# When SyncE asks for V tiles, U tiles and gates in the last stage of a decoder block's expert layer

## The chip, the cores and the metric

The kernel runs on one core of a Trainium2 chip, as one launch. The metric is the device time of that launch in microseconds (us), the median of three runs. Engines are named as the profile does: PE is TensorE, DVE VectorE, ACT ScalarE, POOL GpSimd, SP SyncE. Here SP does nothing but issue transfers, in the order of its program: an issue that waits for a buffer holds all that stand behind it. POOL gathers rows from DRAM (indirect DMAs, on a queue of its own). All transfers share 16 DMA engines.

## The reference

One block of a hybrid decoder on 512 tokens of width 1024: three token mixers side by side (an attention with forget gates, a sliding-window attention and a memory attention), merged by gates and projected, and then a layer of 128 x 128 = 16384 single-neuron experts, of which each token uses 16 for each of 8 heads. The last part is what matters here:

```python
x = x + merged @ w_out[l]
x = x + peer_ffn(rmsnorm(x, norm2_g[l]), ...)
# in peer_ffn, for each token c and its 128 chosen experts e_c, with gates g_c:
a = jnp.einsum('cd,ced->ce', h_c, u[e_c])
act = jax.nn.gelu(a, approximate=False) * g_c
return jnp.einsum('ce,ced->cd', act, v[e_c])
```

## The kernel before

The 512 tokens are four blocks of 128. Blocks 0 and 1 do the experts by rows: POOL fetches the rows of u, and later of v, that each token chose (L833, one row of 4 KB a token, 128 tokens at a time), and DVE multiplies them with the token (L843, tile `scr`) or adds them up weighted (L852, tile `mg`). Blocks 2 and 3 (256 tokens) do the experts densely, over all 16384, in 128 tiles of 128 experts each:

- a U tile (`dense_u`, 512 KB of uT): PE multiplies it with the tokens and ACT takes the gelu into `ga`, the activations of that tile. Two of three U tiles go to PE as plain fp32 (L968). The third is "split": ACT casts it to fp32r (`uhi`, L955), DVE takes the rest (`ulo`, L957), and PE does three cheaper passes.
- the gates of a tile: DVE multiplies `ga` by them (L1079). Those of tiles 0 to 31 stay in SBUF and are multiplied in as they arise; those of the other tiles are written to DRAM (`gd`) and read back four tiles at a time into `gq` (L1061), of which there are two buffers.
- a V tile (`dense_v`, 512 KB of peer_v, into `raw` or, for every fourth, `last`): ACT casts it (`whi`, L1084) and the activations (`ah`, L1082), DVE takes the rests (`wlo`, L128, and `al`, L1087), and PE adds 12 matmuls of 512 columns to four accumulators (tiles `sc` and `tp`, L142 to L144).

The last stage, "beside V", is the loop over k = 0 to 127 in which V tile k is multiplied. Before it 57 or 58 of the U tiles are done; the others are spread over the loop, and so are the remaining row steps of blocks 0 and 1 (`step()`). An iteration runs the first half of `operands(k + 1)` (loads, gates, casts), begins a U tile where one is due, does row steps, takes `ulo` of a split U tile, runs the second half of `operands` (`wlo`, `al`), multiplies the U tile begun one iteration earlier and asks for the U tile three ahead, and multiplies V tile k. There are four buffers for V loads: tile k + 4 takes that of tile k, which is free once `wlo` of tile k has been computed. U tiles have three buffers, all in the tile `hhi` in this stage. The order on POOL, DVE and PE is that of the program from the dense part on (`manual_schedule`, L996 in the kernel before); that on ACT, and before the change that on SP, is chosen by the scheduler of the tile framework.

Of the kernel before, what the change touches and what calls it, by code (L numbers as in the profile page):

```python
# [36 lines left out]
U_SPLIT = 3  # L37
VFAR = 3
PLAIN_ROWS, V_EARLY = 12, 5
GQ_AT, GQ_PARTS = 0, 4  # L40
RAW_MORE = 5
STEPS_U = 4
SPARE, STEPS_N = 4, 0.8
# [4 lines left out]
GK = 4  # L48
# [8 lines left out]
def tile_block(ctx: ExitStack, tc: tile.TileContext, t: dict, out: bass.AP):  # L57
# [61 lines left out]
    def rest(loaded, pool):  # L119
        raw, hi, n, c = loaded  # L120
        w = raw.shape[1]
        lo = wp.tile([128, WSLOT], F32R, tag="wlo", name="wlo")[:, :w]
        due[0] += pool
        if due[0] >= 1.0:
            due[0] -= 1.0
            G.tensor_tensor(lo, raw, hi.bitcast(F32), op=OP.subtract)
        else:
            V.tensor_sub(lo, raw, hi.bitcast(F32))  # L128
        if c > 1:
            return [x.rearrange("p (c n w) -> p n c w", c=c, n=n) for x in (hi, lo)]  # L130
        return [x.rearrange("p (n w) -> p n w", n=n) for x in (hi, lo)]
# [790 lines left out]
    def ga(k):  # L922
        s = k % (LAG + 1)
        return soon[:, s] if s <= LAG - GA_LATE else late[0][:, s - (LAG + 1 - GA_LATE)]
# [21 lines left out]
    def dense_u(k):  # L946

        if k < FIRST_U:
            w = load_raw(t["uT"][k], D)[:, :D]
        else:  # L950
            fetch_u_to(min(k + URING - 1, LAG + 1) if k < LAG else k)
            w = u_raw.pop(k)
        if split_u(k):
            hi, lo = (gp[0].tile([128, D], F32R, tag=tag, name=tag, bufs=1) for tag in ("uhi", "ulo"))
            A.copy(hi, w)  # L955
            yield
            V.tensor_sub(lo, w, hi.bitcast(F32))  # L957
            yield
            ps, hi, lo = bank("mm"), *(x.rearrange("p (n w) -> p n w", n=KC) for x in (hi, lo))
            for dc in range(KC):  # L960
                mm3(ps[:, :TD], (hi[:, dc], lo[:, dc]), [x[dc] for x in h2s], dc == 0, dc == KC - 1)
            A.activation(ga(k), ps[:, :TD], AF.Gelu)
            return
        w = w.rearrange("p (n w) -> p n w", n=KC)
        yield
        ps = bank("mm")
        for dc in range(KC):
            PE.matmul(ps[:, :TD], w[:, dc], h2f[dc], start=dc == 0, stop=dc == KC - 1)  # L968
            yield
        A.activation(ga(k), ps[:, :TD], AF.Gelu)  # L970
# [80 lines left out]
    def get_gates(k, part):  # L1051

        k -= k % GK
        if not KEPT <= k < NK or not 0 <= part < GQ_PARTS:
            return
        if part == 0:
            gq["raw"] = gp[0].tile([128, ND, 128 // TG, GK * TG], F32, tag="gq", name="gq")
            gq[k] = gq["raw"].rearrange("p i g (k t) -> p (i g) k t", k=GK)
        n = ND * (128 // TG) // GQ_PARTS
        i, g = divmod(part * n, 128 // TG)  # L1060
        nc.sync.dma_start(gq["raw"][:, i, g:g + n], gd[i][:, g:g + n, k * TG:(k + GK) * TG])  # L1061

    def fetch_v(k):
        if k < NK:
            pool, n = (gp[0], 1) if k % SPARE == SPARE - 1 else (wp, None)
            tag = "last" if n else "raw"
            raw = pool.tile([128, D if n else WSLOT], F32, tag=tag, name=tag, **({"bufs": n} if n else {}))
            v_raw[k] = raw[:, :D]
            nc.sync.dma_start(v_raw[k], t["peer_v"][k * NK:(k + 1) * NK])

    def operands(k):

        fetch_v(k + VFAR)
        get_gates(k + GK, k % GK - GQ_AT)
        raw, a = v_raw.pop(k), ga(k)
        if k >= KEPT:
            m = gq[k - k % GK][:, :, k % GK]
            g = a.rearrange("p (g t) -> p g t", t=TG)
            V.tensor_mul(g, m, g)  # L1079
        ah = gp[0].tile([128, TD], F32R, tag="ah", name="ah")  # L1080
        al = gp[0].tile([128, TD], F32R, tag="al", name="al")
        A.copy(ah, a)  # L1082
        hi = wp.tile([128, WSLOT], F32R, tag="whi", name="whi")[:, :D]
        A.copy(hi, raw)  # L1084
        yield
        w = [x[:, 0] for x in rest((raw, hi, 1, 1), 0.0)]
        V.tensor_sub(al, a, ah.bitcast(F32))  # L1087
        yield w, ah, al

# [65 lines left out]
    while k_u < LAG:  # L1155
        list(dense_u(k_u))
        k_u += 1
    start, ready = done[0], list(operands(0))[1]
    assert start >= 2 * NJ
    nc.sync.dma_start(out[0:128], x1[0])  # L1160
# [5 lines left out]
    for k in range(NK):  # L1166
        now, coming, us = ready, operands(k + 1) if k + 1 < NK else None, begun
        if coming:
            next(coming)
        begun = []  # L1170
        while k_u < min(NK, LAG + (NK - LAG) * (k + 1) // (NK - 5)):
            begun.append((dense_u(k_u), k_u))
            next(begun[-1][0])
            k_u += 1
        while done[0] < min(len(JOBS), start + (len(JOBS) - start) * (k + 1) // (NK - 4)):
            step()
        for u, n in begun:
            if split_u(n):
                next(u)
        ready = next(coming) if coming else None  # L1180
        for u, n in us:
            list(u)
            fetch_u_to(n + URING_V)
        dense_v(k, *now)
# [96 lines left out]
```

## Time and profile before

| what | us |
|---|---|
| median of three runs | 1624.09 (1624.01 to 1626.73) |
| the profiled execution, its own time | 1624.32 |
| its span on the chip | 1622.5 |
| PE busy | 1545.8 (95%) |
| DVE busy | 1394.1 (86%) |
| ACT busy | 769.1 (47%) |
| POOL busy | 790.5 (49%) |

The mean granted clock of PE was 0.981. The transfers moved 531.83 MB at a mean of 328 GB/s; SP's queue and POOL's moved nearly all of it, 249.12 and 268.47 MB. Busy shares are means over stages with different limits, so they are read by stage; the last stage runs from about 1005 us to the end. A row of the timeline gives the start, the duration, the engine, the line and the operation, and in brackets how long the engine had been idle before it and what released it. "SPq" rows are issues of transfers: the duration is that of the issue, not of the transfer.

### The profile page before, as it was taken

To read this page: it belongs to the slowest core of one execution; us is meant where nothing else is said; L and a number is where in the kernel's file an instruction comes from. 1 tells how busy PE (TensorE), PEld (TensorE's weight loads), DVE (VectorE), ACT (ScalarE), POOL (GpSimd) and SP (SyncE) were. 2 spreads that over 40 slices of the span, in tenths; PEclk is the share of its full clock that TensorE was granted. 3 is DMA by queue.
4 is the path that set the end of the run, shared out by engine and by line. 5 is a ranking of instruction groups with operands and counts; after the bars stand their busy time and mean duration, and the time that the engine had idled before them with its cause. 6 is when DMAs were issued, how large, how long until landed. Compare 5 with 4: busy or idle time off the path is not lost.

```text
span 1622.5 us, 26255 instructions
## 1 busy us (share of the span) xinstructions
PE 1545.8 (95%) x8934; PEld 1382.1 (85%) x8934; DVE 1394.1 (86%) x2709; ACT 769.1 (47%) x1770; POOL 790.5 (49%) x625
## 2 busy tenths in 40 slices
PE   6999999999998989987999999899999999998998
PEld 5999899998887988987888998688888888887887
DVE  5677358899988999999998999788899888897987
ACT  7787337645445434543117878333333333333332
POOL 1100012767556555678553332566555555555652
PEclk9999999999998999999999999999999999999999
DMA  7586743899998899867997999999999999999995
GB/s 298 197 276 219 252 162 131 319 356 319 339 317 296 294 345 347 291 212 258 348 393 286 362 386 335 402 399 379 390 397 402 397 400 402 401 401 401 383 400 220
DMA packets 178101, 531.83 MB, mean 328 GB/s; under 512 B 18224, under 2 KB 47152, under 8 KB 177968
## 3 DMA queue, kind: packets, MB, share of 16 engines
q0 software_dynamic: 73728, 268.47, 44.4%
q1 hardware_dynamic: 100784, 249.12, 42.1%
q10 hardware_dynamic: 3456, 12.58, 2.0%
q8 instruction: 70, 1.15, 0.3%
q14 instruction: 63, 0.52, 0.1%
HBM read 515.42 MB, written 14.68 MB: 327 GB/s over the span
## 4 chain that ended last, share of the span: by engine, by line
PE 51%; DMA 17%; issue 14%; POOL 9%; DVE 8%; ACT 2%; SPq 0%; POOLq 0%; DVEq 0%; ACTq 0%
PE mm L968 15%; DMA row<-in_peer_v_dram,eidx 9%; POOL row L833 8%; PE mm L143 5%; PE mm L142 5%; PE mm L144 5%; DMA row<-in_peer_u_dram,eidx 3%; PE mm L295 2%; DVE wlo L128 2%; DVE scr L843 2%; PE sc L1038 2%; PE tp L1038 2%; PE sc L143 1%; PE sc L144 1%; PE tp L144 1%
## 5 line engine op out<-in xcount | busy, mean ns | idle before, releaser
L833 POOL DMA_INDIRECT row<-in_peer_v_dram,eidx x256 | 351.2, 1372 | 280.8 <-DVE mg L852 157.3
L833 POOL DMA_INDIRECT row<-in_peer_u_dram,eidx x256 | 334.9, 1308 | 266.4 <-DVE scr L843 155.0
L128 DVE TENSOR_TENSOR wlo<-raw,whi 128x1024 fp32r<-128x1024 f32 (+1 forms) x243 | 305.7, 1259 | 44.4 <-ACT whi L116 34.9
L843 DVE SCALAR_TENSOR_TENSOR scr<-row,own 128x1024 bf16<-128x1024 f32 x256 | 314.5, 1229 | 23.1 <-DMA row<-in_peer_u_dram,eidx 20.1
L852 DVE SCALAR_TENSOR_TENSOR mg<-row,acts,mg 128x1024 f32<-128x1024 f32 x237 | 304.4, 1284 | 10.7 <-DMA row<-in_peer_v_dram,eidx 6.8
L968 PE MATMUL mm<-h2f,hhi 128*128 128x256 f32 x1168 | 266.3, 379 | 0.0
L968 PEld LDWEIGHTS mm<-h2f,hhi 128*128 128x128 f32 x1168 | 218.9, 190 | 30.0
L116 ACT CAST whi<-raw 128x1024 fp32r<-128x1024 f32 (+1 forms) x148 | 154.8, 1049 | 93.7 <-PE mm L143 38.7
L189 POOL TENSOR_TENSOR rsy<-rsv,mhalf 128x4 f32<-128x4 f32 (+5 forms) x25 | 39.3, 1576 | 218.2 <-DVE rsv L188 126.2
L1084 ACT CAST whi<-raw 128x1024 fp32r<-128x1024 f32 x96 | 100.5, 1047 | 71.5 <-DMA raw<-in_peer_v_dram 50.1
L142 PE MATMUL sc<-whi,ah 128*128 128x512 f32 x256 | 110.7, 433 | 11.3 <-ACT ah L1082 6.7
L142 PE MATMUL mm<-hhi,whi 128*128 128x384 f32 x320 | 111.1, 348 | 8.0 <-ACT ga L970 6.8
L970 ACT ACTIVATE ga<-mm 128x256 f32<-128x256 f32 x95 | 36.4, 383 | 172.0 <-PE mm L968 165.7
L143 PE MATMUL mm<-hlo,whi 128*128 128x384 f32 x320 | 111.5, 348 | 0.0
L144 PE MATMUL mm<-hhi,wlo 128*128 128x384 f32 x320 | 110.6, 346 | 0.0
L142 PE MATMUL mm<-whi,hhi 128*128 128x256 f32 (+1 forms) x360 | 104.6, 292 | 3.0 <-DVE g L572 1.9
L143 PE MATMUL sc<-wlo,ah 128*128 128x512 f32 x256 | 102.2, 399 | 4.6 <-DVE wlo L128 4.6
L143 PE MATMUL mm<-wlo,hhi 128*128 128x256 f32 (+1 forms) x360 | 103.1, 287 | 0.9 <-DVE wlo L128 0.9
L1082 ACT CAST ah<-ga 128x256 fp32r<-128x256 f32 x116 | 46.7, 405 | 118.6 <-PE tp L143 73.8
L144 PE MATMUL sc<-whi,al 128*128 128x512 f32 x256 | 102.3, 399 | 0.0
L144 PE MATMUL mm<-whi,hlo 128*128 128x256 f32 (+1 forms) x360 | 101.8, 285 | 0.0
L142 PE MATMUL tp<-whi,ah 128*128 128x512 f32 x256 | 101.4, 396 | 0.0
(289 smaller groups left out, 3780.7 us busy)
## 6 DMA issues: line engine op xcount, KB each, us to landing
hhi<-in_uT_dram SPq DMA_DIRECT2D x96, 512.0 KB
raw<-in_peer_v_dram SPq DMA_DIRECT2D x96, 512.0 KB
raw<-in_w_tr_dram SPq DMA_DIRECT2D x48, 512.0 KB
raw<-in_w_nat_dram SPq DMA_DIRECT2D x40, 512.0 KB
last<-in_peer_v_dram SPq DMA_DIRECT2D x32, 512.0 KB
raw<-in_w_o_dram SPq DMA_DIRECT2D x24, 512.0 KB
hlo<-in_uT_dram SPq DMA_DIRECT2D x24, 512.0 KB
gd<-st ACTq DMA_DIRECT2D x24, 512.0 KB
```

What stands on the lines that cost most here:

```text
L116: A.copy(hi[:, :n * w], raw[:, :n * w])
L128: V.tensor_sub(lo, raw, hi.bitcast(F32))
L142: PE.matmul(ps, lh, rh, start=first, stop=False)
L143: PE.matmul(ps, lh, rl, start=False, stop=False)
L144: PE.matmul(ps, ll, rh, start=False, stop=last)
L833: G.indirect_dma_start(out=r, out_offset=None, in_=t["peer_" + tab], in_offset=bass.IndirectOffsetOnAxis(ap=eidx[b][:, j:j + 1], axis=0))
L843: V.scalar_tensor_tensor(scr, r, 1.0, h2n[b], op0=OP.mult, op1=OP.mult, accum_out=acts[b][:, c]))
L852: V.scalar_tensor_tensor(x1[b], r, acts[b][:, c], x1[b], op0=OP.mult, op1=OP.add))
L968: PE.matmul(ps[:, :TD], w[:, dc], h2f[dc], start=dc == 0, stop=dc == KC - 1)
L1038: PE.matmul(ps[:, u], o[:, 1, u], o[:, 0, u], start=True, stop=True)
L1082: A.copy(ah, a)
L1084: A.copy(hi, raw)
```

## The change

```diff
-GQ_AT, GQ_PARTS = 0, 4
+GQ_PARTS = 2
...
     def operands(k):
 
-        fetch_v(k + VFAR)
-        get_gates(k + GK, k % GK - GQ_AT)
+        if k % GK == 0:
+            for part in range(GQ_PARTS):
+                get_gates(k + GK, part)
         raw, a = v_raw.pop(k), ga(k)
...
         w = [x[:, 0] for x in rest((raw, hi, 1, 1), 0.0)]
+        fetch_v(k + VFAR + 1)
         V.tensor_sub(al, a, ah.bitcast(F32))
         yield w, ah, al
...
+    ctx.enter_context(tc.manual_schedule(engines={mybir.EngineType.Pool, mybir.EngineType.DVE, mybir.EngineType.PE,
+                                                  mybir.EngineType.SP}))
+    fetch_v(VFAR)
     start, ready = done[0], list(operands(0))[1]
```

`VFAR` is 3 and `GK` is 4. From the start of the last stage SP, too, issues in program order. A V tile's load stands right after the `wlo` (`rest`) that frees its buffer, instead of at the head of `operands` of the tile after. The gates of a group of four tiles are read by two transfers of 256 KB (one for each token block) at the head of the group before, instead of by four of 128 KB, one in each of the four iterations of the program; the bytes and the buffers are the same. PE's, DVE's and POOL's orders are unchanged.

SP's order at the start of the stage, from the load of V tile 2 on. `raw` and `last` are V tiles (2, 3, 4, ...), `hhi` are U tiles, `gq` gates. Before:

```order
L1069 DMA raw_10752<-in_peer_v_dram 128x1024
L934 DMA hhi_8910<-in_uT_dram 128x1024
L1069 DMA last_10924<-in_peer_v_dram 128x1024
L1061 DMA gq_12009<-gd0_8904 128x2x128 x2
L1069 DMA raw_10953<-in_peer_v_dram 128x1024
L1061 DMA gq_12009<-gd1_8905 128x2x128
L934 DMA hhi_8910<-in_uT_dram 128x1024
L1061 DMA gq_12152<-gd0_8904 128x2x128 x2
L1061 DMA gq_12152<-gd1_8905 128x2x128
L1069 DMA raw_10983<-in_peer_v_dram 128x1024
```

And now:

```order
L1069 DMA raw_10752<-in_peer_v_dram 128x1024
L1069 DMA last_10926<-in_peer_v_dram 128x1024
L1069 DMA raw_10935<-in_peer_v_dram 128x1024
L1165 DMA out_0_dram<-mg0_2246 128x1024
L1069 DMA raw_10968<-in_peer_v_dram 128x1024
L1069 DMA raw_11002<-in_peer_v_dram 128x1024
L1069 DMA last_11032<-in_peer_v_dram 128x1024
L1069 DMA raw_11062<-in_peer_v_dram 128x1024
L1069 DMA raw_11092<-in_peer_v_dram 128x1024
L934 DMA hhi_8910<-in_uT_dram 128x1024 x3
```

The gates of the first two groups (tiles 32 to 39) have gone from here: their reads now stand behind V tiles 31 and 35. U tile 59, which stood behind V2, and the two after it stand behind V9. The store of the first token block to `out` has come in behind V4.

SP's order further on, from the load of V tile 101 on. Before, the U tiles in these rows are 115, 116 and 117 and the last V tile is 105:

```order
L1069 DMA raw_14842<-in_peer_v_dram 128x1024
L1069 DMA raw_14872<-in_peer_v_dram 128x1024
L934 DMA hhi_8910<-in_uT_dram 128x1024
L1061 DMA gq_14919<-gd0_8904 128x2x128 x2
L1061 DMA gq_14919<-gd1_8905 128x2x128 x2
L934 DMA hhi_8910<-in_uT_dram 128x1024
L1069 DMA last_14917<-in_peer_v_dram 128x1024
L1069 DMA raw_14975<-in_peer_v_dram 128x1024
L1069 DMA raw_15005<-in_peer_v_dram 128x1024
L934 DMA hhi_8910<-in_uT_dram 128x1024
```

And now, where the U tiles are 114, 115 and 116 and the last V tile is again 105:

```order
L1069 DMA raw_14786<-in_peer_v_dram 128x1024
L934 DMA hhi_8910<-in_uT_dram 128x1024
L1069 DMA raw_14826<-in_peer_v_dram 128x1024
L1069 DMA last_14859<-in_peer_v_dram 128x1024
L934 DMA hhi_8910<-in_uT_dram 128x1024
L1061 DMA gq_14885<-gd0_8904 128x4x128
L1061 DMA gq_14885<-gd1_8905 128x4x128
L1069 DMA raw_14902<-in_peer_v_dram 128x1024
L934 DMA hhi_8910<-in_uT_dram 128x1024
L1069 DMA raw_14958<-in_peer_v_dram 128x1024
```

U tile 116, a split one, stood directly behind four gate reads and V102; it now stands behind two gate reads and V104.

ACT's order at the same place, from the cast of V tile 102 on. `whi` are the casts of V tiles, `ah` those of activations, `uhi` that of U tile 116. Before:

```order
L1084 CAST whi_15012<-raw_14872 128x1024
L1082 CAST ah_14979<-ga_7513 128x256
L955 CAST uhi_15086<-hhi_8910 128x1024
L970 ACTIVATE late_9433<-mm_15023 128x256
L1082 CAST ah_15009<-ga_7513 128x256
```

And now:

```order
L1085 CAST whi_14977<-raw_14826 128x1024
L1083 CAST ah_14945<-ga_7513 128x256
L1085 CAST whi_15017<-last_14859 128x1024
L1083 CAST ah_14974<-ga_7513 128x256
L970 ACTIVATE late_9433<-mm_14990 128x256
L1085 CAST whi_15049<-raw_14902 128x1024
L1083 CAST ah_15014<-ga_7513 128x256
L955 CAST uhi_15051<-hhi_8910 128x1024
```

The cast of U tile 116 stood behind that of V102; it now stands behind that of V104.

## The prediction

> **What bounds the kernel now.** I read the page first, for what is busy; then the windows by stage, for which limit holds where; then SP's own timeline at the start of the last stage, because the change acts on SP's queue; then the waits and the ten-microsecond windows where that stage stumbles. The page (busy us, share of the span, instructions; then GB/s in 40 slices of 40.6 us):
>
> ```profile
> PE 1545.8 (95%) x8934; PEld 1382.1 (85%) x8934; DVE 1394.1 (86%) x2709; ACT 769.1 (47%) x1770; POOL 790.5 (49%) x625
> GB/s 298 197 276 219 252 162 131 319 356 319 339 317 296 294 345 347 291 212 258 348 393 286 362 386 335 402 399 379 390 397 402 397 400 402 401 401 401 383 400 220
> ```
>
> PE looks like the bound, but from the 26th slice on the transfers stand at some 400 GB/s without a gap. The windows of the last stage (length, then busy time of PE, weight loads, DVE, ACT and POOL; granted clock, DMA share, GB/s):
>
> ```profile
> 1005.00:1043.00 38.00, 30.21 (x129) 23.63 (x128) 30.06 (x52) 12.68 (x25) 18.70 (x13) 0.91 1.01 382
> 1043.00:1146.00 103.00, 103.00 (x506) 88.14 (x505) 87.94 (x133) 37.67 (x60) 62.82 (x42) 1.00 1.00 391
> 1146.00:1590.00 444.00, 432.72 (x2103) 366.95 (x2102) 394.12 (x511) 163.22 (x258) 255.83 (x170) 0.99 1.03 397
> 1590.00:1622.50 32.50, 28.55 (x126) 23.27 (x125) 23.90 (x31) 8.96 (x14) 4.79 (x3) 0.97 0.49 180
> ```
>
> Four parts. A start (38 us) in which neither PE nor DVE is full. A part of 103 us with PE busy all of it, when gates still lie in SBUF. A long part of 444 us in which the DMA share is 1.03 and PE has 11 us of gaps: there the bytes set the pace. A tail in which DMA runs dry. The subtraction at L1087 runs once per V tile:
>
> ```profile
> 1043.00:1146.00 103.00, 9.72 (x23) 1.00 1.00 391
> 1146.00:1590.00 444.00, 38.25 (x91) 0.99 1.03 397
> ```
>
> So a step takes 103/23 = 4.5 us where PE sets it and 444/91 = 4.88 us where the bytes do. Nothing in the change takes a byte or a matmul away: the change can only gain where DMA or PE now stand idle, or lose by making them idle.
>
> **The start.** SP's timeline (start, length of the issue) and what waits for it:
>
> ```profile
> 1004.16 0.33 SPq L934 DMA_DIRECT2D hhi<-in_uT_dram  x1
> 1017.17 3.04 SPq L1061 DMA_DIRECT2D gq<-gd  x3
> 1020.31 0.42 SPq L1069 DMA_DIRECT2D raw<-in_peer_v_dram  x1
> 1022.38 0.87 SPq L1061 DMA_DIRECT2D gq<-gd  x2
> 1024.29 2.16 SPq L1069 DMA_DIRECT2D raw<-in_peer_v_dram  x1
> ...
> 1011.03 1.23 DVE L128 TENSOR_TENSOR wlo<-raw,whi 128x1024 fp32r<-128x1024 f32 x1
> ...
> 1024.06 1.22 DVE L128 TENSOR_TENSOR wlo<-raw,whi 128x1024 fp32r<-128x1024 f32 x1
> ...
> 1033.12 1.04 ACT L1084 CAST whi<-raw 128x1024 fp32r<-128x1024 f32 x1 [9.03 <-DMA raw<-in_peer_v_dram]
> ...
> 1034.20 1.22 DVE L128 TENSOR_TENSOR wlo<-raw,whi 128x1024 fp32r<-128x1024 f32 x1 [6.11 <-ACT whi L1084]
> 1038.09 1.22 DVE L957 TENSOR_TENSOR ulo<-hhi,uhi 128x1024 fp32r<-128x1024 f32 x1
> ...
> 1040.34 0.34 PE L142 MATMUL mm<-hlo,uhi 128*128 128x256 f32 x1
> ...
> 1043.27 0.39 PE L142 MATMUL sc<-whi,ah 128*128 128x512 f32 x1
> ```
>
> The load issued at 1020.31 is V5, that at 1024.29 V6; the wlo rows are those of tiles 1, 4 and 5. V5's buffer was free when wlo of tile 1 ended, at 1011.03 + 1.23 = 1012.26; it is asked for 8.05 us later, behind reads of gates that nobody needs before tile 32. DVE then waits 6.11 us for the cast of V5. After the change V5 to V9 stand first, each behind the wlo that frees its buffer, so V5 is asked for at about 1012.3. With the same flight as now (1020.31 to the cast at 1033.12, 12.8 us) it is there at 1025.1, while wlo of tile 4 is just done (1025.28). The 6.11 us go.
>
> What is late next is a U tile. The first row of the fence, at 1004.16, asks for U59, the first split one of the stage; after the change it and the two behind it stand after V9, whose buffer comes free with wlo of tile 5. Without the wait that wlo ends near 1029.3 (1025.28, then 0.43 for al, two row multiplications of 1.23 us as an estimate, and its own 1.22). U59 is then asked for near 1029.7 instead of 1004.16, and ulo, its split on DVE, stands ahead of the wlo of tile 6. When does it land? At the soonest V9 and U59, 0.5 MB each, need 2.6 us apiece at some 200 GB/s for SP's half of the traffic (fence below), so about 1033; at the latest after V5's 12.8 us, 1042.5. I take 1036, nearer to the soonest since no gates stand in the queue then. With a cast of 1.04, ulo of 1.22 and 2.9 us of U59's matmuls (now 1040.34 to 1043.27), the matmuls of tile 6 begin at 1036 + 5.2 = 1041.2 instead of 1043.27: **-2.1 us**, bounds -5.1 (1033) and +4.4 (1042.5). So the wait changes its name more than it goes.
>
> The two gate groups now read in this start, 1.05 MB, are read later, behind V31, at the border of the long part. There they cost 1.05 MB / 0.397 MB per us = 2.6 us if bytes set the pace, and nothing if PE does (103.00 busy of 103). Both limits stand within 0.4 us a step there; I take the half, **+1.3 us**, bounds 0 and +2.6.
>
> **The gates in the long part.** Queues from 1160 to 1590 (packets, MB, share of 16 engines), then two windows of 4 us, the first with gates being read and the second without:
>
> ```profile
> q1 hardware_dynamic: 44133, 85.05, 52.6%
> q0 software_dynamic: 23578, 85.87, 50.6%
> ...
> DMA packets 961, 1.52 MB, mean 381 GB/s; under 512 B 80, under 2 KB 662, under 8 KB 961
> q0 software_dynamic: 317, 1.16, 75.6%
> q1 hardware_dynamic: 644, 0.36, 30.0%
> ...
> q1 hardware_dynamic: 277, 1.00, 61.9%
> ```
>
> q1 is SP's queue (85.05 MB in 430 us, 198 GB/s), q0 POOL's rows. While gates pass, SP's queue gets 0.36 MB in 4 us, 90 GB/s: two of its packets of about 560 B (0.36 MB / 644) for each of POOL's of 3.7 KB. A group of four tiles' gates, 0.52 MB, so holds SP's queue for about 5.8 us, and what stands behind it waits. In two places before that is a split U tile:
>
> ```profile
> 1478.91 3.10 SPq L1061 DMA_DIRECT2D gq<-gd  x4
> 1482.59 4.93 SPq L934 DMA_DIRECT2D hhi<-in_uT_dram  x1
> 1487.62 1.31 SPq L1069 DMA_DIRECT2D last<-in_peer_v_dram  x1
> ...
> 1498.76 1.04 ACT L955 CAST uhi<-hhi 128x1024 fp32r<-128x1024 f32 x1 [8.77 <-DMA hhi<-in_uT_dram]
> ...
> 1500.41 0.43 DVE L1087 TENSOR_TENSOR al<-ga,ah 128x256 fp32r<-128x256 f32 x1 [5.98 <-ACT ah L1082]
> ...
> 1490.00:1500.00 10.00, 5.77 (x26) 4.54 (x25) 4.37 (x5) 1.24 (x3) 3.04 (x3) 0.89 1.03 406
> 1500.00:1510.00 10.00, 9.57 (x34) 7.96 (x35) 9.42 (x13) 4.52 (x8) 4.47 (x3) 0.77 1.01 369
> 1510.00:1520.00 10.00, 10.00 (x57) 8.67 (x56) 9.89 (x12) 3.23 (x6) 6.09 (x5) 1.00 0.99 381
> 1520.00:1530.00 10.00, 10.00 (x47) 8.42 (x46) 8.70 (x11) 4.80 (x7) 5.85 (x5) 1.00 1.01 367
> ...
> 1560.08 3.74 SPq L934 DMA_DIRECT2D hhi<-in_uT_dram  x1
> ...
> 1576.51 1.04 ACT L955 CAST uhi<-hhi 128x1024 fp32r<-128x1024 f32 x1 [2.64 <-DMA hhi<-in_uT_dram]
> 1577.89 0.43 DVE L1087 TENSOR_TENSOR al<-ga,ah 128x256 fp32r<-128x256 f32 x1 [5.82 <-ACT ah L1082]
> ...
> 1570.00:1580.00 10.00, 10.00 (x47) 8.56 (x47) 4.15 (x6) 2.87 (x5) 1.68 (x1) 1.00 1.03 412
> ```
>
> U116 is asked for right behind a group and is there 16 us later; ACT stands 8.77 us at its cast, with ah queued behind it, and DVE waits 5.98 us for ah. DVE then frees no buffers, so the next 30 us move 369, 381 and 367 GB/s. Against the stage's 397 and the 406 ahead of them that is 0.28 + 0.16 + 0.30 - 0.09 = 0.65 MB, 1.6 us lost. U125 at 1560 does the same at the end, where DMA soon runs dry (0.49 in the tail), so DVE's 5.82 us count between nothing and all; the bytes did flow meanwhile (412 GB/s), so I take a quarter, 1.5. After the change no gate read stands directly ahead of those two tiles: a V load stands between, and the cast of U116 comes after that of V104 on ACT instead of V102. I take both as gone: **-3.1 us**, bounds -7.4 (1.6 + 5.8) and 0.
>
> By the Trainium skill ("DMA: Bandwidth & Descriptors", Queues, rings and completion order) a DMA engine takes a whole packet of typically 9 to 17 descriptors from one queue before it turns to the next. The trace shows about two small ones to a turn (644 against 317).
>
> **The rest at nothing.** SP issues two gate reads instead of four for the same bytes, 48 fewer in all; SP's waits are for buffers, not for its own time:
>
> ```profile
> SPq L1069 <- DVE wlo L128: 96.5, 47, 4.7
> ```
>
> Its cover is DMA's full queue; if that ran empty, 0.8 us an issue (3.10/4) would show. V loads in the long part already leave as their buffer comes free, so their new place is worth nothing there. The store of out[0:128], 0.5 MB, moves from ahead of the stage to behind V4: up to 1.3 us of bytes at the start, inside the range. DVE's, PE's and POOL's orders are as before.
>
> **Sum**, against the profiled execution's own 1624.32 us (span 1622.5; the median of three is 1624.09): 1624.3 - 2.1 + 1.3 - 3.1 = 1620.4; I say 1620. Some 0.2%, 3.2 us, is what a measurement can tell from no change, so this is just beyond it.
>
> **Rivals.**
>
> 1. Nothing measurable. DMA was at 1.01 and 382 GB/s even in the start, so what V5 gains there some later transfer loses, and the stalls move to other tiles. For it: the shares above 1.00 in three parts. Against: 382 and the dips to 367 are under 397. Time: 1624.3 - 0 to 2 = 1622 to 1625.
>
> 2. A larger gain. U59 lands at 1033 and both stalls go with the whole of their DVE time: 1624.3 - 5.1 + 1.3 - 5 = 1615.5; 1613 to 1618. Against: a DMA queue that is full cannot give back DVE's idle time.
>
> 3. Slower: split U tiles become late everywhere. Each is now asked for one or two tiles of V later than before (U116 behind V104 instead of V102), while DVE's order, in which its ulo stands ahead of wlo of tile 104, stays. From the gates' issue at 1478.91 to the cast at 1498.76 passed 19.9 us; with one V load more in the queue (0.52 MB / 0.198 = 2.6 us) it is 22.5. DVE comes to that ulo 4.6 steps after, 4.6 x 4.88 = 22.4. So it stands on the edge: from 3 us later on, DVE stops at each of the tiles so placed (U86, U95, U116, U125: each behind a gate group and one V), at the price of the 1490 stall, 1.6 us, in three and 3 us in the last, 7.8, of which 3.1 are there today: 1624.3 - 2.1 + 1.3 + 4.7 = 1628; with more such tiles up to 1632. If U59 itself takes 12.8 us, +4.4 in the start instead of -2.1, the same side is reached with smaller stalls.
>
> 4. Gates are not what held U116. If a group passed at the rate that SP's queue has on the whole, 198 GB/s, it would be through after 2.6 us, and U116 would have been late for another reason, which remains: the -3.1 falls away, 1623.5 us. The two small packets to a turn in the window at 1467, and its 90 GB/s, speak against it; I give it 0.06. By the rule of the Trainium skill above, the group's 64 packets per engine would go in four to seven turns, which is this case.
>
> **Chances.** The forecast with its own range of 1618 to 1621.5: 0.34. The larger gain: 0.14. No change, with the fourth: 0.30. Slower: 0.22. The forecast case falls below 1620.8 in three parts of four, so faster is 0.25 + 0.14 + some of the no-change cases' lower edge, 0.43; same is 0.34; slower than 1627.3 is 0.23 with the edge of the first rival. For eight in ten the range reaches from within the larger gain, 1614, to within the slower case, 1629.
>
> **What would show it.** V5 asked for at about 1012; no 6 us wait of DVE for tile 5's cast, but one for ulo of U59, with tile 6's matmuls near 1041. Gate reads in pairs, behind the loads into "last". No wait of 8 us of ACT for a U tile near 1490 and 397 to 400 GB/s there. Wrong: waits of ulo on uhi all through the long part, steps above 4.88 us, a DMA share under 1.00 there, or U59 landing after 1040.

## The result, and the profile after

The change made the kernel slower: 1637.67 us median of 10 runs (1630.47 to 1642.9) against 1627.15 us of 10 runs of the kernel before (1624.01 to 1631.96); ratio 1.0065, interval 1.0048 to 1.0082. The three runs known before the change lay at the lower end of what the kernel before does, so ratios are read rather than medians. The profiled execution of the changed kernel has a span of 1636.3 us, 13.8 more than before's 1622.5.

The windows of the last stage of the changed kernel, in the columns of the prediction's:

```profile
1005.00:1043.00 38.00, 26.30 (x115) 21.46 (x115) 25.54 (x47) 12.43 (x34) 15.65 (x12) 0.87 0.78 275
1043.00:1146.00 103.00, 96.59 (x464) 82.44 (x463) 83.08 (x124) 36.00 (x57) 58.31 (x39) 0.97 0.98 378
1146.00:1590.00 444.00, 432.05 (x2103) 366.45 (x2102) 392.84 (x514) 163.03 (x257) 254.30 (x170) 1.00 1.03 398
1590.00:1622.50 32.50, 32.50 (x158) 27.64 (x156) 28.34 (x33) 11.77 (x19) 10.52 (x8) 1.00 0.88 342
```

The long part is as it was (398 GB/s, 2103 matmuls in 444 us, before 397 and 2103). The loss lies in the first two windows. In the first, DMA's share is 0.78 instead of 1.01, 275 GB/s instead of 382, and PE and DVE each do 4 us less; in the second, PE does 6.4 us less. What stands in the first is the stall that the prediction did not have, and in the second the wait for U59. SP's timeline, then DVE's, PE's and ACT's rows of the changed kernel:

```profile
1008.10 0.33 SPq L1069 DMA_DIRECT2D last<-in_peer_v_dram  x1
1009.56 0.33 SPq L1069 DMA_DIRECT2D raw<-in_peer_v_dram  x1
1009.94 0.47 SPq L1165 DMA_DIRECT2D out_dram<-mg  x1
1025.54 4.21 SPq L1069 DMA_DIRECT2D raw<-in_peer_v_dram  x2
...
1009.79 1.42 DVE L138 TENSOR_TENSOR hlo<-h2f,hlo 128x256 fp32r<-128x256 f32 x4
1021.80 1.43 DVE L138 TENSOR_TENSOR mg<-h2f,hlo 128x256 fp32r<-128x256 f32 x4 [10.60 <-DMA out_dram<-mg]
...
1025.57 0.80 PE L143 MATMUL sc<-wlo,ah 128*128 128x512 f32 x1 [11.50 <-DVE wlo L128]
...
1050.12 1.04 ACT L955 CAST uhi<-hhi 128x1024 fp32r<-128x1024 f32 x1 [3.70 <-DMA hhi<-in_uT_dram]
1051.20 1.22 DVE L957 TENSOR_TENSOR ulo<-hhi,uhi 128x1024 fp32r<-128x1024 f32 x1 [7.22 <-ACT uhi L955]
...
1057.03 0.39 PE L142 MATMUL sc<-whi,ah 128*128 128x512 f32 x1
```

The third row is the store of out[0:128]. It reads the tile `mg0`, in which the first token block's result lies, and the same tile is given to half of the low parts of the tokens' transposes (`h2s`, `wide("mg0", 1, F32R)`), which DVE writes at the start of the stage. So DVE's four writes into `mg` wait until the store has landed, 11.8 us after its issue: 10.60 us of idle DVE, with every `wlo` behind it, so V5 is asked for at 1025.54 instead of 1012, and PE waits 11.50. Before, the scheduler had issued that store at 934.7 us. The second wait is the one that was foretold: 7.22 us of DVE for the cast of U59. The last row is the first matmul of V tile 6, 13.76 us later than before's 1043.27. Of these, 2.61 us stood already at V tile 0 (1010.74 against 1008.13). Two profiles of one and the same kernel further down (store and U59 early) differ there by 2.8 us (1010.12 and 1012.94), so this part is not put down to the change.

To read the experiments I use two lengths of each profile: the start, from the first matmul of V tile 0 to that of tile 6, and the rest, from there to the end of tile 127; both come from one profile of each kernel. Before: 1043.27 - 1008.13 = 35.1 and 1618.55 - 1043.27 = 575.3 us. After: 46.3 and 1632.34 - 1057.03 = 575.3. The whole change is in the start, +11.2 us.

### The profile page after: what moved, and what is told of

The parts are those of the page before. It is cut to its first block, busy times and chain, and to the rows that moved or that the text cites. A ratio compares the mean times of both kernels' runs of the same rounds, so it can differ in the third digit from the quotient of the medians.

```text
span 1636.3 us, 26141 instructions
## 1 busy us (share of the span) xinstructions
PE 1545.2 (94%) x8934; PEld 1382.6 (84%) x8934; DVE 1394.1 (85%) x2709; ACT 769.2 (47%) x1770; POOL 787.3 (48%) x625
## 4 chain that ended last, share of the span: by engine, by line
PE 33%; issue 19%; DMA 19%; DVE 15%; POOL 12%; ACT 2%; SPq 0%; POOLq 0%; DVEq 0%; ACTq 0%
POOL row L833 11%; DMA row<-in_peer_v_dram,eidx 9%; DMA row<-in_peer_u_dram,eidx 8%; PE mm L968 7%; PE mm L143 5%; PE mm L142 5%; PE mm L144 5%; DVE o L1023 4%; DVE scr L843 3%; DVE mg L852 3%; PE mm L295 2%; DVE wlo L128 2%; PE sc L494 1%; DMA raw<-in_uT_dram 1%; DMA raw<-in_w_skvf_dram 1%
## 5 line engine op out<-in xcount | busy, mean ns | idle before, releaser
L833 POOL DMA_INDIRECT row<-in_peer_v_dram,eidx x256 | 345.0, 1348 | 284.2 <-DVE mg L852 157.2
L143 PE MATMUL sc<-wlo,ah 128*128 128x512 f32 x256 | 102.1, 399 | 13.8 <-DVE wlo L128 13.8
```

The costliest lines, as they stand in the source:

```text
L143: PE.matmul(ps, lh, rl, start=False, stop=False)
L833: G.indirect_dma_start(out=r, out_offset=None, in_=t["peer_" + tab], in_offset=bass.IndirectOffsetOnAxis(ap=eidx[b][:, j:j + 1], axis=0))
```

## The experiments

Theory S says that the store, by DVE's wait for its tile, is the loss; rival L that it is the U tiles asked for late, U59 and the split ones after it.

**The store early.** Edit to the changed kernel:

```diff
+    nc.sync.dma_start(out[0:128], x1[0])
     ctx.enter_context(tc.manual_schedule(engines={..., mybir.EngineType.SP}))
     fetch_v(VFAR)
     start, ready = done[0], list(operands(0))[1]
-    nc.sync.dma_start(out[0:128], x1[0])
```

> The change, with the store of out[0:128] issued before SP's fixed order begins, so that it goes out as early as in the kernel before. Theory S (DVE's 10.6 us wait for the store, whose tile mg it is to write, is the whole loss): that wait is gone, V5 is asked for near 1012, and the time is within 3 us of the kernel before (ratio 0.998 to 1.001). Rival L (the loss comes from U59 and the other split U tiles being asked for late): the time stays 6 us or more above before (ratio 1.004 or more), with a wait of DVE for uhi of U59 of 5 us or more and others like it later.

Measured: ratio 1.0015 (0.9999 to 1.0031). The wait for the store is gone; start 36.6, rest 575.1. What is left of U59 shows on SP, ACT, DVE and PE:

```profile
1031.64 1.63 SPq L934 DMA_DIRECT2D hhi<-in_uT_dram  x3
...
1039.16 1.04 ACT L955 CAST uhi<-hhi 128x1024 fp32r<-128x1024 f32 x1 [3.79 <-DMA hhi<-in_uT_dram]
...
1040.24 1.22 DVE L957 TENSOR_TENSOR ulo<-hhi,uhi 128x1024 fp32r<-128x1024 f32 x1 [6.25 <-ACT uhi L955]
...
1040.26 0.58 PE L142 MATMUL mm<-hlo,uhi 128*128 128x256 f32 x1 [6.04 <-ACT uhi L955]
...
1045.97 0.39 PE L142 MATMUL sc<-whi,ah 128*128 128x512 f32 x1
...
1040.00:1043.00 3.00, 2.28 (x9) 1.99 (x10) 2.76 (x4) 0.20 (x1) 0.00 (x0) 0.50 0.91 365
```

U59 comes 7.5 us after its issue, DVE and PE wait 6 us for it, and then PE works at a granted clock of 0.50 (the last row's third number from the right), so U59's 24 matmuls take 5.7 us (1040.26 to 1045.97, with a wait of 0.46 for `ulo` in it) instead of 2.9. By time, 8 of the change's 10.5 us were the store's. Theory S holds as far as the store's wait goes; that it is the whole loss does not, for the wait for U59 is still there, and the next run shows its price.

**The store early, and U59 early.** The same, with one more line, so that U59 is asked for ahead of V3 as before:

```diff
+    fetch_u_to(LAG + 2)
     fetch_v(VFAR)
```

> As the run with the early store, and U59 asked for ahead of V3, as in the kernel before. Theory S: the 7.2 us wait of DVE for the cast of U59 goes too; a gain of 2 to 5 us over the run with the early store alone, ratio to before 0.996 to 0.999. If the bytes set the pace even in the start, the wait goes and the time does not (within 1 us of the run with the early store).

Measured: ratio 0.9952 (0.9938 to 0.9965), and measured a second time 0.9955 (0.9938 to 0.9973). Start 29.0, rest 574.3; tile 6's first matmul and the window of the start:

```profile
1039.07 0.39 PE L142 MATMUL sc<-whi,ah 128*128 128x512 f32 x1
...
1005.00:1043.00 38.00, 34.17 (x163) 27.31 (x162) 34.32 (x58) 15.90 (x36) 21.33 (x15) 1.00 1.00 381
```

PE and DVE each do 4 us more in the start than before at nearly the same 381 GB/s. So the early V loads, with the gates out of their way, bring 35.14 - 28.95 = 6.2 us, U59's delay takes 36.56 - 28.95 = 7.6 away, and the store's wait 46.29 - 36.56 = 9.7; -6.2 + 7.6 + 9.7 = +11.1 is the change.

> The kernel with early store and early U59 a second time, beside the one that reads no gates: ratio to before 0.993 to 0.997 as before.

**U59 early, the store late** (only the line above, the store behind V4 as in the change):

> The change with U59 asked for ahead of V3, but the store of out[0:128] left where the change put it, behind V4. Theory S (DVE's wait for the store and DVE's wait for U59 are two separate losses that add): U59's wait goes, the store's of 10 us stays; 8 to 12 us above the run with both mended, so 1627 to 1631, some 6 to 9 us under the change. If the two waits overlapped (one stall, named twice), mending one would bring nothing: 1636 or more.

Measured: 1629.82 us, ratio 1.0011 (0.9998 to 1.0025), start 38.7:

```profile
1023.15 1.43 DVE L138 TENSOR_TENSOR mg<-h2f,hlo 128x256 fp32r<-128x256 f32 x4 [10.90 <-DMA out_dram<-mg]
```

The store alone costs 38.74 - 28.95 = 9.8 us, U59 alone 46.29 - 38.74 = 7.6: the same two numbers as from the other side, so the two waits add and do not cover one another.

**The store late, the writes into `mg` later.** The loop that splits the tokens' transposes does its first half where it was and the second, which writes `mg`, at k = 3:

```diff
-    for dc in range(KC):
+    for dc in range(KC // 2):
         split(h2s[0][dc], h2s[1][dc], h2f[dc])
...
+        if k == 3:
+            for dc in range(KC // 2, KC):
+                split(h2s[0][dc], h2s[1][dc], h2f[dc])
```

> The change with the store where the change put it, behind V4; only the second half of the splitting of the tokens' transposes (the four writes into mg) is done three iterations later, when the store has landed. Theory S: DVE no longer waits for the store, time within 3 us of the run with the early store. If it is the store's 0.5 MB in SP's queue rather than DVE's wait that costs, the time stays near that of the change (ratio 1.005 or more).

Measured: ratio 1.0011 (0.9999 to 1.0022), start 37.4, the writes at 1025.72 without a wait:

```profile
1025.72 1.42 DVE L138 TENSOR_TENSOR mg<-h2f,hlo 128x256 fp32r<-128x256 f32 x4
```

With the store's 0.5 MB still behind V4, the time is that of the early store. It is DVE's wait that cost, not the bytes, which is the only way in which the prediction counted the store.

**The store on ACT's queue** (`nc.scalar.dma_start` in the same line):

> The change with the store of out[0:128] at the same place of the program but issued by ACT on its own queue, U59 as in the change. If the store takes 11.8 us to land because V3 and V4, 1 MB, stand ahead of it in SP's queue, it lands some 5 us sooner and DVE's wait falls from 10.6 to 5 us or so: 1632 to 1634. If the time is the store's own, or the wait is for its place in the program, the wait stays at 9 to 11 us and the time at 1636 to 1640.

Measured: ratio 1.0009 (0.9993 to 1.0025), start 36.5. It does not tell what it was made for: ACT's order is the scheduler's, which moved the store ahead of the stage (to 940.1 us), so there was no wait left to shorten. The changed kernel's own trace says more. What SP's queue (q1) and ACT's (q10) move from 1009 to 1022 us:

```profile
q1 hardware_dynamic: 432, 1.57, 34.4%
q10 hardware_dynamic: 432, 1.57, 29.6%
```

SP's 1.57 MB are V3, V4 and the store; ACT's are three writes of gates to `gd`, issued from 1008.7 us on. V4, issued 0.4 us ahead of the store, lands 9.7 us after its issue, and the store 2.5 us after V4. So most of the 11.8 us passed behind V3 and V4, beside ACT's writes; that an emptier queue would shorten the wait was not tested.

**SP's order left to the scheduler** (the call of `manual_schedule` at the start of the stage taken out, all else as in the change):

> The change without the fixed order on SP: gates read in pairs and V loads placed behind wlo in the program, but the scheduler orders SP. The store goes out early and the first two groups of gates are read in the start again. Theory S: as before within 3 us (ratio 0.998 to 1.002). Rival L: since U tiles are asked for as early as before, also as before; so it does not tell S from L, but shows whether the pairs of gate reads by themselves cost or bring anything.

Measured: ratio 0.998 (0.9969 to 0.999), start 30.2, rest 576.0. The program's new places for the V loads and the gate reads bring most of the gain in the start (30.2 against 35.1 before and 29.0 above) even without a fixed order, with U59 and the store where the scheduler had them.

**Two groups of gates ahead of V3** (early store and U59; the reads of tiles 32 to 39 called ahead of `fetch_v(VFAR)`):

> Early store and early U59, with the first two groups of gates (tiles 32 to 39, four reads of 256 KB) asked for right ahead of V3, none of them needed before tile 32. If a group holds SP's queue for 5.8 us (the rate of 90 GB/s seen while gates pass), V3 lands 8 us or more later, PE and DVE wait for it, and the time is 4 to 8 us above the run without them. If a group passes at the queue's usual 198 GB/s (2.6 us), V3 is 5 us later and just in time: within 2 us.

Measured: 1627.02 us, ratio 0.9993 (0.9978 to 1.0009), some 6 to 7 us above the two measurements of the run without; start 37.3. SP, DVE waiting for V3, then what SP waited for, and what its queue moved from 1014.7 to 1018.7:

```profile
1006.09 10.62 SPq L1061 DMA_DIRECT2D gq<-gd  x4
1016.76 0.81 SPq L1069 DMA_DIRECT2D last<-in_peer_v_dram  x1
...
1028.03 1.23 DVE L128 TENSOR_TENSOR wlo<-last,whi 128x1024 fp32r<-128x1024 f32 x1 [8.53 <-ACT whi L1085]
...
SPq L1061 <- DMA gd<-st: 7.9, 1, 7.9
...
q1 hardware_dynamic: 605, 0.30, 27.0%
```

The time is where a slow group was to put it, but by another wait: of the 10.62 us, 7.9 are SP's wait until ACT's write of these same gates to `gd` has landed, and the last three reads are issued only from 1014.75 on. V3, asked for at 1016.76 instead of 1007.48, stands behind that wait. So the run does not price a group's small pieces. What it does show is that SP's queue is slow while they pass, 0.30 MB in 4 us or 75 GB/s beside ACT's writes and POOL's rows, where the window at 1467 had 90. How long one group holds the queue is not measured. The rule of the Trainium skill ("DMA: Bandwidth & Descriptors", Queues, rings and completion order), whole packets of typically 9 to 17 descriptors to a turn, is not tested either: the counts of pieces and rows (644 to 317 in the prediction's window) are a ratio of two queues and do not tell how many pieces a turn holds. The next runs ask what the small pieces cost over the stage.

**The gates in pieces of 2 KB** (early store and U59):

```diff
-    gd = [dram.tile([128, 128 // TG, NK * TG], F32, ...
+    gd = [dram.tile([128, NK // GK, 128 // TG, GK * TG], F32, ...
...
-                nc.scalar.dma_start(gd[i][:, t0 // TG, k0 * TG:(k0 + SPILT) * TG], ...
+                nc.scalar.dma_start(gd[i][:, k0 // GK:(k0 + SPILT) // GK, t0 // TG], ...
...
-        nc.sync.dma_start(..., gd[i][:, g:g + n, k * TG:(k + GK) * TG])
+        nc.sync.dma_start(..., gd[i][:, k // GK, g:g + n])
```

> Early store and early U59, with the gates laid out in DRAM so that a group's read is one run of 2 KB per partition and token block instead of four of 512 B (the writes, on ACT's queue ahead of the last stage, become pieces of 512 B instead of 4 KB). If small packets hold SP's queue and the transfers bound the long part, the windows with gate reads go from 388 to about 405 GB/s, a step from 4.88 to about 4.75 us, and the time falls by 4 to 9 us against the run with early store and U59, less what the small writes cost before. If the gate reads are hidden, within 2 us of it or slower by the writes.

Measured: 1623.23 us (1613.28 to 1635.31), ratio 0.9975 (0.9947 to 1.0003), so in all nothing is gained over early store and U59 (0.9952 and 0.9955). The rest falls from 574.3 to 564.3 us; the long part, beside the run with early store and U59:

```profile
1146.00:1590.00 444.00, 440.29 (x2151) 374.97 (x2150) 403.75 (x523) 166.39 (x263) 259.71 (x175) 1.00 1.03 408
```
```profile
1146.00:1590.00 444.00, 434.23 (x2111) 368.85 (x2111) 397.52 (x513) 163.10 (x257) 252.31 (x170) 0.99 1.03 398
```

The transfers go at 408 instead of 398 GB/s, with the same DMA share of 1.03. But the stage begins 12.9 us later than in that run (V tile 0 at 1023.02 against 1010.12): ACT, which issues the writes, now in 512 B pieces, stood four times with nothing that the profile shows to wait for (880 to 1020 us):

```profile
ACT o L1026 <- issue: 20.0, 4, 9.2
```

**The writes issued by SP, and by both** (the same kernel; `nc.sync` for all 24 writes, or ACT for one of three and SP for two):

> As the run with 2 KB pieces of gates, with the 24 writes of the gates (512 B pieces) issued by SP instead of ACT. In the run before, ACT stood four times 5 to 9 us before an operation of the spreading (20 us in all, with nothing released that the profile shows), while it issued these writes; the last stage began 13 us later than with 4 KB writes. If holding ACT is the cost, SP takes it over, the last stage begins within 4 us of the kernel before, and the time is 1608 to 1613. If the small writes' share of DMA is the cost, or SP's U loads come late behind them, the stage begins as late as before: 1619 or more.

> The same with one of three writes issued by ACT and two by SP: two queues share them. If it is the holding of one issuer, ACT is held a third as long: 1609 to 1614; if it is DMA's time, no better than with all on ACT, 1619 or more.

Measured: 1613.65 us, ratio 0.9911 (0.9893 to 0.9929), and 1611.23 us, ratio 0.9906 (0.9887 to 0.9925). Both are some 15 us under the kernel before, and their intervals overlap. The rest is 565.0 and 564.2 us, and ACT's 20 us of waiting are gone in both. The stage begins at 1014.83 with SP alone, not within the 4 us of before's 1008.13 that were expected, and at 1008.05 with both; the kernels with the old layout begin it anywhere from 1008.13 to 1013.49, so little of that difference is shown to be the issuer's. The Trainium skill (same page, Rules for kernel authors) has it that spreading DMAs over issuing engines brings no bandwidth and only saves the issuer's time; these two runs agree: from 880 to 1005 us the transfers move 360 GB/s with SP alone and 362 with both, 365 in the kernel before, and what is saved is ACT's waiting.

**No gate reads.** Early store and U59, old layout; the gates of tiles 32 to 39 serve all later tiles, so the kernel leaves out the other gates and does not compute the block:

> Early store and early U59, with the gates of tiles 40 to 127 not read: those of tiles 32 to 39 are used again and again (this leaves 11.5 MB of the transfers of the last stage out; the arithmetic keeps its amount). If the stalls of the long part (14.7 us over the best pace in every kernel so far, at tiles that differ) are what the gates' transfers cost, they go almost all: 1605 to 1609, and the run with 2 KB pieces, 3.8 us, had already saved three quarters of it. If the bytes, not the small pieces, were the cost, leaving them out saves far more than the 10.9 us that the 2 KB pieces saved: 25 us or more (11.5 MB at 0.4 MB per us is 29 us) if nothing else binds.

Measured: 1605.09 us, ratio 0.9866 (0.9846 to 0.9886); rest 559.4 us, 14.9 less than with all reads. In its long part DMA is no longer full and PE is:

```profile
1146.00:1590.00 444.00, 443.83 (x2173) 379.32 (x2172) 409.42 (x528) 168.29 (x266) 264.37 (x170) 1.00 0.98 379
```

So the gates' reads cost 14.9 us in the rest, and their small pieces 10.0 of these (574.3 - 564.3); with the second profile of early store and U59, whose rest is 573.6, it is 14.2 and 9.3. That is two thirds, where three quarters were expected. Leaving the reads out brings no more than this because PE then sets the pace, at 443.83 of 444.

## Why the prediction was wrong, point by point

**The step that failed is the store.** It was put as "up to 1.3 us of bytes at the start", inside the range. By its bytes it costs at most 0.8 us (start 37.4 with the store behind V4 and no wait, 36.6 with the store early); what counts is that a store also holds the tile that it reads, and that DVE writes that tile at the start of the stage. That wait measured 9.7 and 9.8 us in the start (46.29 - 36.56, and 38.74 - 28.95). Both facts stood in the shown code: `wide("mg0", ...)` and the store of `x1[0]`, with SP's order showing it behind V4. Set on the forecast's base of 1624.3, the ratio of 1.0065 gives 1634.9 us, above the range's end of 1629; with the store early, 1.0015 gives 1626.7, inside it.

**The start without the store, -2.1 foretold, +1.4 measured** (36.56 - 35.14). The V loads came as said: DVE's 6.11 us wait for V5 is gone, worth -6.2 once U59 is early too. With the first matmuls of V tile 0 laid on one another (1009.41 with the store early, 1008.13 before), tile 6 begins at 1044.7 where 1041.2 was foretold, 3.5 us later. Of these, 0.7 are that U59 was asked for later, 1.2 that it came 7.5 us after its issue where 6.3 was taken, and 1.6 that 6.8 us passed from there to tile 6 instead of 5.2. The last is the largest: PE, idle for 6 us, came back at a granted clock of 0.50, and U59's matmuls took 5.7 us for the 2.9 counted, while `ulo`, counted ahead of them, ran beside them. The soonest landing, "about 1033", was too early by the prediction's own figures: two loads of 2.6 us from 1029.3 on end at 1034.5. The bound of +4.4 covered all this. U59's delay cost 7.6 in all, more than the V loads bring.

**The gates moved out of the start, +1.3, and the stalls at U116 and U125, -3.1: together -1.8 foretold, 0.0 measured.** The rest is 575.3 us before and after. To see where it goes, I take the best pace: for each step from one V tile to the next, the shortest time that it took in five profiles (before, after, store early, store and U59 early, gates in 2 KB pieces). The stall at 1490 did go: the kernel before lost 4.8 us against the best pace in the step of tile 101 and 2.1 in that of 102, and the changed kernel nothing there. But it lost 4.1 at tile 82 and 2.3 at tile 109 instead. All eight profiles with a fixed order on SP and reads in 512 B pieces stall there, by 3.0 to 4.9 us at tile 82, while the kernel whose SP order was left to the scheduler stalled at 101 and 102, as before. In the changed kernel SP, ACT and DVE show what is late at tile 82:

```profile
1400.10 1.20 SPq L1061 DMA_DIRECT2D gq<-gd  x2
1403.56 5.91 SPq L1069 DMA_DIRECT2D raw<-in_peer_v_dram  x2
...
1421.04 1.04 ACT L1085 CAST whi<-raw 128x1024 fp32r<-128x1024 f32 x1 [4.87 <-DMA raw<-in_peer_v_dram]
...
1422.42 0.42 DVE L1089 TENSOR_TENSOR al<-ga,ah 128x256 fp32r<-128x256 f32 x1 [5.42 <-ACT ah L1083]
```

The step of the sum that failed here is "a V load stands between". It does, and now it is late itself: V84, asked for right behind the two gate reads, is cast 17.5 us after its issue, with `ah` queued behind the cast on ACT and DVE waiting 5.42 us for `ah`. With the gates in 2 KB pieces the step of tile 82 is 0.8 us over the best pace, and without gate reads it is at the best pace.

In the windows of 10 us of the run with early store and U59:

```profile
1400.00:1410.00 10.00, 6.17 (x23) 5.12 (x24) 6.16 (x9) 2.71 (x4) 3.66 (x2) 0.66 1.04 391
1410.00:1420.00 10.00, 10.00 (x53) 8.67 (x52) 9.89 (x13) 3.47 (x6) 6.22 (x5) 1.00 0.99 349
...
1490.00:1500.00 10.00, 10.00 (x47) 8.46 (x46) 7.81 (x8) 2.42 (x5) 5.96 (x5) 1.00 1.05 397
1500.00:1510.00 10.00, 10.00 (x57) 8.77 (x56) 8.99 (x11) 4.31 (x7) 3.06 (x3) 1.00 1.04 396
```

The picture of 1490 before, PE at 5.77 and then 369 GB/s, stands at 1400 here. In the ten profiles with reads in 512 B pieces the rest stays between 573.5 and 576.0 us, whatever SP's order: in this stage, whose transfers are full, the order said at which tile DVE waited and hardly how much. Over all steps from tile 28 on the excess over the best pace is 14.7 us before, 14.7 after and 13.7 with early store and U59, and 3.8 where the gates come in large pieces. The first rival said it ("the stalls move to other tiles"), at 0.30 together with the fourth.

**The third rival had the sign by the right neighbour.** U59 late was in it, as an addition; the split tiles that it meant in the long part did not cost. From 1060 us on DVE waited 0.2 us in all for the cast of a split U tile in the changed kernel:

```profile
DVE ulo L957 <- ACT uhi L955: 0.2, 1, 0.2
```

The range ended at 1629; what lay outside was the store. The fourth rival, that a group would pass in 2.6 us, does not follow from a count of turns, since nothing here gives the time of a turn.

**Right:** V5 asked for near 1012 (1013.57 with the store early), the wait moving from V5's cast to U59's, V loads and pairs of gate reads worth nothing in the long part (rest 576.0 with both, SP's order left to the scheduler), and SP's queue slow while small gate pieces pass (90 GB/s in the prediction's window, 75 in the run with gates ahead of V3). That a group so holds the queue for 5.8 us is not shown.

## What to carry to other kernels

When a queue's order is fixed by hand, list every transfer that the scheduler had placed early, stores too, and ask of each which tile it reads or fills and who next writes that tile: a store is priced by that wait, not by its bytes. Where one load is moved ahead, name the load that it overtakes and the engine that needs it (here one line each gave back 9.7 and 7.6 us). A read that is moved ahead can itself wait, for the write that fills its source, and hold the queue meanwhile (7.9 us here). In this stage, whose transfers were full, a stall that went at one tile showed up at another, and only fewer bytes or larger pieces shortened it.

## What the hardware showed that was not expected

The granted clock: with the store early, after 6 us of waiting, PE ran at 0.50 and took 2.8 us more for 24 matmuls (0.21 us apart in place of 0.12 in the run without the wait; 0.46 of it was a wait for `ulo`), so a wait of PE cost more than a third of itself again. The kernel before shows the same after PE's wait of 4.56 us for V5, in the 12 matmuls of tile 5, 0.43 us apart in place of 0.23:

```profile
1034.20:1040.30 6.10, 5.62 (x12) 4.14 (x13) 6.07 (x8) 2.68 (x5) 2.83 (x2) 0.50 1.03 410
```

And the pieces of 512 B: the Trainium skill ("DMA: Bandwidth & Descriptors", Specifications) gives 512 B as the least for line rate; here 512 B pieces beside 4 KB rows held the long part to 398 GB/s and 2 KB pieces gave 408, worth 9 to 10 us of the stage, so at 512 B the full engines were not yet at their best rate.
